# Weight blocks stored contiguously in memory and loaded from GpSimd's queue

## The chip, the cores and the metric

The kernel runs on one core of a Trainium2 chip. The metric is the device time of one execution in microseconds; lower is better. The profile shows the engines by short names: PE is TensorE's matmul, PEld its weight load, DVE is VectorE, ACT is ScalarE, POOL is GpSimd, and SP is the sync engine, which computes nothing and starts transfers. Every engine works through its own row of instructions in order and waits where an operand or a buffer isn't ready.

## The reference

The model is a trunk of two layers over 1024 tokens of 1024 channels in float32. Layer 0 mixes the tokens by an RG-LRU and a gated DeltaNet side by side (the even mixer), layer 1 by HGRN2 and RWKV-7 (the odd mixer). Each layer then has a gated feed-forward net and a gated embedding term:

```python
for layer in range(2):
    hn = rms_norm(h, norm_mix[layer])
    h = h + mixer(hn @ w_in[layer]) @ w_out[layer]        # even or odd
    f = rms_norm(h, norm_ffn[layer])
    h = h + (silu(f @ ffn_w_gate[layer]) * (f @ ffn_w_up[layer])) @ ffn_w_down[layer]
    g = sigmoid(rms_norm(h, norm_ple[layer]) @ ple_w_gate[layer])
    h = h + g * (p[layer] @ ple_w_up[layer])
return rms_norm(h, norm_final)
```

The weights e_w_in, e_w_out, o_w_in, o_w_out, the three of the feed-forward net and the two of the embedding term are the large ones. All products are to float32's accuracy.

## The kernel before

The tokens are worked on in two halves of 512. A large product is made from weight blocks of 128 x 1024 floats (8 tiles of 128 channels by 128 columns; in ffn_w_down 4 or 3 tiles of channels by 256 columns; 512 KB, twelve of them 384 KB). There are 450 blocks over the program. `weights` (line 1168) allots the tile wraw for a block (three buffers) and loads it by `load` (line 151), that is, from SP's queue. The weight lies in memory as the reference has it, so a block is 1024 pieces of 512 bytes, 8 for each of 128 partitions (for ffn_w_down pieces of 1 KB). Then the block is split: ACT copies it to whi, which holds the high part (line 304), and DVE subtracts that and leaves the low part in wlo (two buffers each). `products` (line 1182) multiplies each operand, itself split (xhi, xlo for the normed input; ghi, glo in the feed-forward net), in three passes: high by high, low by high, high by low. One pass of 128 x 128 weights over 512 tokens is one matmul of PE.

The order of each engine's row is set when the program is built. Every instruction gets a planned time (`at`, `clock`: loads 28,700 of the planner's units ahead of the product, splits 40,000), and a list scheduler with a model of the engines and queues picks the next instruction for each engine by it. So a change of a transfer's modelled time or queue can move instructions on all engines. The mixers of one half are spread over the dense products of another stage and fill the row of PE between them with small products, whose outputs are called mx.

Both mixers contain the inverse of many triangular 32 x 32 blocks (`invert_blocks`, line 480; eight times in the program, four for DeltaNet and four for RWKV-7). Their blocks are written to memory (scr, from aq or pm), and one load of 512 KB brings them back as lane, with one small system on each partition; L copies of a system lie on L partitions, so the source has a broadcast dimension. DVE then eliminates step by step (w<-lane,cols and cols<-cols,w), and the result goes through memory once more (invt) to the products that use it (`gdn_inverse`, line 511, and `r7_inverse`). Small transfers of all kinds (z, the mixers' inputs and outputs; up, the embedding term; hspill) use SP's queue too, in one row with the weights.

Of the kernel before, what the change touches and what calls it, by code (L numbers as in the profile page):

```python
# [19 lines left out]
P = 128  # L20
D = 1024
KD = D // P
# [6 lines left out]
# Planned times order the instructions: a pass of 512 tokens through the array takes PASS, the dense stages  # L29
# run from START on, and what they need is planned ahead of them by  # L30
PASS, START = 216, 100000
FETCH, WSPLIT = 28700, 40000    # weights: load, split
SPLIT, EARLY = 12000, 60000     # a mixer's output and other inputs
EVAC = 45000                    # what takes products out of the accumulators
# the second half's first operands; starts and ends of the mixers, against the dense stages around them
# [3 lines left out]
# a mixer's matrix products against its other instructions, and more behind a way through memory  # L39
LAG, ILAG = 7000, 4000  # L40
# shares and numbers of instructions of the parts of a mixer
# [18 lines left out]

class Trunk:
    def __init__(self, ctx, tc, ins, out):
        self.tc, self.nc = tc, tc.nc
        self.ins, self.out = ins, out
        self.const = ctx.enter_context(tc.tile_pool(name="const", bufs=1))
# [34 lines left out]
    def at(self, t, step=0, lag=0):  # L100
        """What follows is issued as if planned for time t, each instruction `step` after the last,
        and matrix products `lag` later, when their operands have long been there."""
        self.tc.cur_priority = max(int(t), 1)
        self.step, self.lag = step, lag
# [50 lines left out]
    def first_constants(self):  # L155
# [9 lines left out]
        # le[s, t] = 1 where s <= t  # L165
# [11 lines left out]
    def columns(self, stacks):  # L177
        """Per-channel vectors: rows of 128 channels, turned into columns."""
# [32 lines left out]
    def even_constants(self):  # L211
# [10 lines left out]
        # softplus(-lambda) = max(-lambda, 0) + ln(1 + exp(-|lambda|)), times 4  # L222
# [17 lines left out]
    def level_mask(self, m, dt):  # L240
        """mask[s, t] = 1 where s lies in the left half and t in the right half of the same block of 2m."""
# [6 lines left out]
        # 0 <= s - 2m*b < m  # L248
# [8 lines left out]
    def odd_constants(self):  # L257
# [13 lines left out]
        # takes the mean of a head's channels off  # L271
        self.cen = c.tile([P, P], F32, name="cen")
        self.stt(self.cen, self.blk, -1.0 / 64, self.ident, ALU.mult, ALU.add)
        # running sums start anew at every chunk
# [5 lines left out]
        # rows: k (64), beta (64); columns: alpha (s < t), r (s <= t)  # L280
# [9 lines left out]
    def rsqrt(self, x, y, t):  # L290
        """y = x ** -0.5, by exp and ln and one Newton step; t is scratch."""
        self.act(y, x, AF.Ln)
        self.act(y, y, AF.Exp, scale=-0.5)
        self.newton(x, y, t)

    def newton(self, x, y, t):
        """One step towards y = x ** -0.5."""
        self.mul(t, x, y)
        self.stt(t, t, -0.5, y, ALU.mult, ALU.mult)
        self.stt(y, t, 1.5, y, ALU.add, ALU.mult)  # L300

    def split(self, src, hi, lo):
        """src = hi + lo, both with the 12 bit significands that one pass of the array carries."""
        self.nc.scalar.copy(hi, src)  # L304
        self.sub(lo, src, hi)

    def rsqrt_cols(self, x):
        """x ** -0.5 of a few columns: half the exponent off the float's integer, then Newton steps."""
# [7 lines left out]
    def inv_mean(self, ps, n, scale, eps):  # L316
        """(scale * sum + eps) ** -0.5 of n columns of sums."""
# [5 lines left out]
    def load_unit(self, z, g, u, halo, tag):  # L323
        """Tokens of one unit with `halo` earlier ones of a group of four channel tiles."""
# [14 lines left out]
    def conv(self, x, w, bias, out):  # L339
        """Causal convolution, tile by tile; w: columns of tap k and tile j."""  # L340
# [12 lines left out]
    def rg_unit(self, z, u, mixed):  # L353
        """In steps, between which other work is issued."""
# [3 lines left out]
        c = self.w4()  # L358
# [15 lines left out]
        # with s = tanh(-log_a / 2): sqrt(1 - a^2) = sqrt(s) (1 + a); half of it, as gelu comes doubled  # L374
# [43 lines left out]
    def gdn_gates(self, ab):  # L418
        """Per half: columns over the tokens of a chunk, [token, chunk, head]."""
# [37 lines left out]
    def conv_silu(self, z, grp, u, out):  # L457
        """Twice silu of the convolved group, into out."""
# [10 lines left out]
    def head_norm(self, src, sq, dst, scale, eps):  # L469
        """dst = src * (scale * sum of sq + eps) ** -0.5, the sums over the 64 channels of a head."""  # L470
# [40 lines left out]
    def gdn_inverse(self, at, side):  # L511
        """Transposed inverses of I + A, at: [s, (chunk, head), t] with the transposes of the strictly lower A."""
# [24 lines left out]
        # pairs of 32: rows 32.. of the first and 96.. of the second  # L537
# [69 lines left out]
    def gdn_unit(self, z, u, cl, mixed, side):  # L607
        """Keys and queries stay as they leave silu (doubled); their norms are factors of the tokens."""
# [14 lines left out]
        # columns [token, chunk, head]  # L623
# [31 lines left out]
        # r * (r^2 mean(o^2) + eps)^-1/2 with r the query's factor, 1/sqrt(d) in it  # L655
# [26 lines left out]
    def gdn_scores(self, c, cc, kq, ks, cl, rk, kdc, aq):  # L682
        """aq: [s, head, (A | q k), t] with the decays exp(gc_t - gc_s), t >= s."""
# [32 lines left out]
    def gdn_chunk(self, c, ks, vb, nbe, o, tinv, qk, qe, kd, egl):  # L716
        """The recurrence over chunks; o: [token, head, channel]."""
# [45 lines left out]
    def hg_unit(self, z, u, mixed):  # L763
# [22 lines left out]
        # scores across the middles of blocks of 2m, by factors that reach to the middle  # L786
        for m in (64, 32, 16, 8, 4, 2, 1):
# [11 lines left out]
            # only the right halves of the blocks receive, in columns [block, token]  # L799
# [14 lines left out]
            else:  # L814
                # one product to a block: sums over the channels, on all partitions
# [78 lines left out]
    def r7_unit(self, z, u, mixed):  # L894
# [9 lines left out]
        # decay: log w = -KAPPA * (1 + tanh(.))  # L904
# [15 lines left out]
        # factors between chunks: exp(b_end - b_mid + next b_mid), and exp(b_mid) at the start  # L920
# [20 lines left out]
        # k * (1 + (a - 1) k_a)  # L941
# [5 lines left out]
        # bonus  # L947
# [56 lines left out]
    def r7_chunk(self, c, ar, bk, v, gs, o, pm, tinv, first):  # L1004
        """The recurrence over chunks; heads of pm and tinv in the order of (parity, pair)."""
# [50 lines left out]
    def fetch(self, hf, spare=False):  # L1056
        """The residual stream of a half, channels on partitions; spare: in the mixers' space."""
# [22 lines left out]
    def first_fetch(self, w):  # L1080
        """The first half of the input and its operands: h, and h * w in two parts."""
# [28 lines left out]
    def norm_scale(self, acc_tile=None):  # L1110
        """The inverse root mean squares of the tokens, on all partitions."""
# [18 lines left out]
    def norm(self, w):  # L1130
        """Operands h * w; the factors of the tokens (norm_scale) go to the products instead."""
# [9 lines left out]
    def even_operands(self, hf, w, alloc):  # L1141
        """Operands of the first projection: the input, normed with tokens on partitions."""
# [25 lines left out]
    def weights(self, w, k0, nk, c0, n):  # L1168
        """One block: raw, and its two parts, [channel, k, column]."""
# [6 lines left out]
        self.load(raw, w[P * k0:P * (k0 + nk), c0:c0 + n].rearrange("(k p) c -> p k c", p=P))  # L1176
# [5 lines left out]
    def products(self, w, k0, nk, c0, n, *sets):  # L1182
        """Yields w[k0.., c..]^T times the operands of each set for each 128 of n columns, to float32's
        accuracy in three passes."""
# [291 lines left out]
```

## Time and profile before

| | us |
|---|---|
| median of 3 runs | 3081.62 (3079.82 to 3084.49) |
| span of the profiled execution | 3078.0 |
| PE busy | 2972.8 (97%) |
| DVE busy | 1958.5 (64%) |
| ACT busy | 1264.2 (41%) |
| POOL busy | 27.5 (1%) |
| mean share of the 16 DMA engines that is busy | 38.8% |

The busy shares are means over the whole span. Times in the trace's views count from the span's start. Behind a row of a timeline stands in brackets how long the engine had been idle ahead of it and what it had waited for; a view of waits sums these idle times. A view of windows gives for a stretch the busy time of the engines, the granted clock of TensorE, the share of the DMA engines that is busy, and the rate.

### The profile page before, as it was taken

Reading aid. Unit: us, or ns where it says so; the run is one execution under the profiler, and the core shown is the slowest. Engines: PE = TensorE matmul, PEld = TensorE weight load, DVE = VectorE, ACT = ScalarE, POOL = GpSimd, SP = SyncE. Lnnn points to the kernel's source line nnn. Section 1 sums busy time; section 2 is a strip of 40 time slices with the busy share of each in tenths; the row PEclk is TensorE's granted clock in tenths of the full one; section 3 lists DMA queues with packets and bytes.
Section 4 is the critical chain, followed back from the end, with each engine's and each line's share of the span. In section 5 each row is a group of like instructions: output and inputs, shape, how many; then the busy total and the mean of one; then the engine's idle time right before and its main releaser. Section 6 shows DMA issues by size and latency. Waiting matters only on the chain.

```text
span 3078.0 us, 39136 instructions
## 1 busy us (share of the span) xinstructions
PE 2972.8 (97%) x15281; PEld 2407.9 (78%) x15281; DVE 1958.5 (64%) x3316; ACT 1264.2 (41%) x1799; POOL 27.5 (1%) x99
## 2 busy tenths in 40 slices
PE   8989899999999999999999999999998999999998
PEld 6878678778878887777877778777787787888886
DVE  5665556556676547745786574565687398555557
ACT  5344554233244436234443452442453355422224
POOL 0000000000000000000000000000000000000000
PEclk9999999999999999999999999999999999999999
DMA  6553663333234554222233444523233235333323
GB/s 207 146 140 110 167 202 100 111 86 103 84 110 137 164 167 149 86 78 91 86 107 93 131 143 136 162 86 79 83 110 89 53 96 181 100 120 99 97 89 103
DMA packets 547423, 360.18 MB, mean 117 GB/s; under 512 B 67287, under 2 KB 508806, under 8 KB 547238
## 3 DMA queue, kind: packets, MB, share of 16 engines
q1 hardware_dynamic: 547238, 357.68, 38.8%
q8 instruction: 120, 1.97, 0.3%
q14 instruction: 65, 0.53, 0.1%
HBM read 298.87 MB, written 58.75 MB: 116 GB/s over the span
## 4 chain that ended last, share of the span: by engine, by line
PE 55%; DVE 7%; DMA 3%; ACT 2%; issue 2%; SPq 0%; ACTq 0%; DVEq 0%
PE acc L144 46%; PE mx L144 8%; DMA lane<-scr 2%; DVE wlo L118 1%; DVE tmp L118 1%; PE mx L149 1%; DVE w L118 1%; DVE pm L118 1%; ACT w L139 1%; DVE w L131 0%; DMA tmp<-mixed 0%; DVE h L131 0%; DVE w L760 0%; ACT whi L304 0%; DVE tmp L131 0%
## 5 line engine op out<-in xcount | busy, mean ns | idle before, releaser
L144 PE MATMUL acc<-xhi,wlo 128*128 128x512 f32 x2864 | 1127.5, 394 | 18.9 <-DVE wlo L118 18.8
L144 PE MATMUL acc<-xhi,whi 128*128 128x512 f32 x2864 | 1137.4, 398 | 4.1 <-ACT xhi L304 2.9
L144 PE MATMUL acc<-xlo,whi 128*128 128x512 f32 x2864 | 1129.6, 395 | 1.0 <-DVE xlo L118 0.9
L304 ACT CAST whi<-wraw 128x1024 fp32r<-128x1024 f32 (+1 forms) x450 | 463.5, 1030 | 1157.1 <-PE acc L144 833.2
L144 PEld LDWEIGHTS acc<-xhi,wlo 128*128 128x128 f32 x2864 | 539.1, 188 | 139.3 <-DVE wlo L118 22.7
L144 PEld LDWEIGHTS acc<-xhi,whi 128*128 128x128 f32 x2864 | 539.4, 189 | 123.4 <-ACT xhi L304 5.4
L144 PEld LDWEIGHTS acc<-xlo,whi 128*128 128x128 f32 x2864 | 539.5, 188 | 119.5 <-issue 4.4
L118 DVE TENSOR_TENSOR wlo<-wraw,whi 128x1024 fp32r<-128x1024 f32 (+1 forms) x450 | 539.4, 1199 | 101.2 <-ACT whi L304 86.9
L118 DVE TENSOR_TENSOR tmp<-acc,rs 128x512 f32<-128x512 f32 (+1 forms) x205 | 140.8, 689 | 363.0 <-PE acc L144 362.6
L144 PE MATMUL acc<-ghi,wlo 128*128 128x512 f32 x704 | 278.7, 396 | 11.1 <-DVE wlo L118 11.1
L144 PE MATMUL acc<-ghi,whi 128*128 128x512 f32 x704 | 281.1, 400 | 2.6 <-ACT whi L304 2.5
L144 PE MATMUL acc<-glo,whi 128*128 128x512 f32 x704 | 277.8, 395 | 0.0
L144 PEld LDWEIGHTS acc<-ghi,wlo 128*128 128x128 f32 x704 | 134.0, 190 | 41.3 <-DVE wlo L118 12.9
L118 DVE TENSOR_TENSOR tmp<-tmp,acc 128x512 f32<-128x512 f32 x88 | 60.4, 686 | 166.4 <-PE acc L144 165.8
L144 PEld LDWEIGHTS acc<-ghi,whi 128*128 128x128 f32 x704 | 134.0, 191 | 32.7 <-ACT whi L304 2.9
L144 PEld LDWEIGHTS acc<-glo,whi 128*128 128x128 f32 x704 | 134.1, 190 | 28.0 <-DVE glo L118 0.6
L139 ACT ACTIVATE w<-w 128x1024 f32<-128x1024 f32 (+2 forms) x116 | 108.6, 940 | 105.3 <-DVE w L118 44.8
L131 DVE SCALAR_TENSOR_TENSOR h<-acc,h 128x512 f32<-128x512 f32 x144 | 98.6, 687 | 66.8 <-PE acc L144 66.3
L139 ACT ACT_TABLE_LOAD x83 | 106.5, 1283 | 5.5 <-DVE w L135 4.1
L118 DVE TENSOR_TENSOR w<-lane,cols 128x30 f32<-128x30 f32 (+43 forms) x248 | 57.5, 232 | 79.7 <-DMA lane<-scr 73.6
L139 ACT ACTIVATE tmp<-tmp 128x512 f32<-128x512 f32 x120 | 75.4, 629 | 54.8 <-DVE tmp L118 54.1
L304 ACT CAST ghi<-tmp 128x512 fp32r<-128x512 f32 x88 | 54.5, 619 | 100.8 <-DVE tmp L118 100.5
(320 smaller groups left out, 2729.0 us busy)
## 6 DMA issues: line engine op xcount, KB each, us to landing
wraw<-in_ffn_w_gate_dram SPq DMA_DIRECT2D x88, 512.0 KB
wraw<-in_ffn_w_up_dram SPq DMA_DIRECT2D x88, 512.0 KB
wraw<-in_ffn_w_down_dram SPq DMA_DIRECT2D x64, 512.0 KB
wraw<-in_o_w_in_dram SPq DMA_DIRECT2D x60, 512.0 KB
wraw<-in_e_w_in_dram SPq DMA_DIRECT2D x48, 512.0 KB
wraw<-in_ple_w_gate_dram SPq DMA_DIRECT2D x32, 512.0 KB
wraw<-in_ffn_w_down_dram SPq DMA_DIRECT2D x32, 384.0 KB
wraw<-in_e_w_out_dram SPq DMA_DIRECT2D x16, 512.0 KB
```

Source lines behind the costliest of these rows:

```text
L118: (eng or self.nc.vector).tensor_tensor(out, a, b, op=op)
L131: self.nc.vector.scalar_tensor_tensor(out, a, s, b, op0=op0, op1=op1)
L139: self.nc.scalar.activation(out, a, f, **kw)
L144: self.nc.tensor.matmul(out, lhsT, rhs, start=start, stop=stop)
L149: self.nc.tensor.transpose(out, a, self.ident)
L304: self.nc.scalar.copy(hi, src)
```

## The change

The host lays each of the nine large weights out anew: block after block in the order in which the kernel loads them, and within a block partition by partition, so that what goes to one partition is one piece of 4 KB (3 KB in the small blocks). `WEIGHTS` lists the blocks, the class `Weights` finds a block's offset, and the load in `weights` reads it as one flat stretch. This load is issued by `nc.gpsimd.dma_start`, from GpSimd's queue; `load`, and so every other transfer, stays with SP. Constants, buffers and planned times are as before; comments are taken out, which moves the line numbers (load is line 201, the weight load line 1226).

```diff
+def column_blocks(nk, n):
+    per = P * (KD // nk)
+    return [(b0, min(per, n - b0)) for b0 in range(0, n, per)]
+
+def in_blocks(order, groups, tails):
+    return [(0, KD, 512 * groups.index(g) + b0 if g in groups else 512 * len(groups) + b0, nb)
+            for g in order for b0, nb in column_blocks(KD, tails.get(g, 4 * P))]
+
+def plain_blocks(nk, n, k0=0, c0=0):
+    return [(k0, nk, c0 + b0, nb) for b0, nb in column_blocks(nk, n)]
...
+class Weights:
+    def __init__(self, ap, blocks):
+        self.ap, self.at, o = ap, {}, 0
+        for k0, nk, c0, n in blocks:
+            self.at[k0, nk, c0, n] = o
+            o += P * nk * n
+
+def laid_out(w, blocks):
+    import numpy as np
+    return np.stack([np.concatenate([
+        l[P * k0:P * (k0 + nk), c0:c0 + n].reshape(nk, P, n).transpose(1, 0, 2).ravel()
+        for k0, nk, c0, n in blocks]) for l in w])
...
         raw = block("wraw", F32, 3)
-        self.load(raw, w[P * k0:P * (k0 + nk), c0:c0 + n].rearrange("(k p) c -> p k c", p=P))
+        o = w.at[k0, nk, c0, n]
+        self.nc.gpsimd.dma_start(raw, w.ap[o:o + P * nk * n].rearrange("(p k c) -> p k c", p=P, c=n))
         self.at(self.clock - WSPLIT)
...
         a = np.ascontiguousarray(inputs[name])
+        if name in WEIGHTS:
+            a = laid_out(a, WEIGHTS[name])
```

The rows of the engines change in their order too. SP's row goes from 904 to 454 entries, POOL's from 85 to 535. On PE, ACT and DVE the same instructions stand in a slightly different order. Three places matter below.

The first is ACT's row at the start of the program, where the operands of the first half (xhi) are made from the transposed input (mx, acc), h is copied aside, and the first two weight blocks (whi_220, whi_251) are split. Before:

```order
L304 CAST whi_220<-wraw_218 128x1024
L139 ACTIVATE xhi_124<-mx_119,cols_95 128x512
...
L1099 COPY h_150<-mx_141 128x512
L139 ACTIVATE xhi_201<-mx_196,cols_95 128x512
L304 CAST whi_251<-wraw_249 128x1024
```

Now:

```order
L188 ACTIVATE xhi_124<-mx_119,cols_95 128x512
...
L188 ACTIVATE xhi_190<-acc_185,cols_95 128x512
L188 ACTIVATE xhi_201<-mx_196,cols_95 128x512
L353 CAST whi_220<-wraw_218 128x1024
L1148 COPY h_172<-acc_163 128x512
L353 CAST whi_251<-wraw_249 128x1024
```

The split of the first block has moved from the head of the row to behind the eighth operand. On PE the second block's first products (acc_255<-xhi_124,whi_251) have moved from the twentieth and twenty-first place of the dense products to the third and fourth.

The second place is PE's row in a stretch of the feed-forward net, where mx_3629 is the first small product on what DeltaNet's third elimination (w, brought back from memory) gives, between the dense products acc. Before:

```order
L144 MATMUL acc_6194<-glo_6078,whi_6190 128x512
L144 MATMUL acc_6194<-ghi_6077,wlo_6191 128x512
L144 MATMUL mx_3629<-w_624_3615,aq_3460 32x32 x8
L144 MATMUL acc_6208<-ghi_5722,whi_6190 128x512
L144 MATMUL acc_6208<-glo_5723,whi_6190 128x512
```

Now:

```order
L193 MATMUL acc_6174<-ghi_5931,wlo_6157 128x512
L193 MATMUL acc_6174<-ghi_6004,whi_6156 128x512
L193 MATMUL mx_3629<-w_624_3615,aq_3460 32x32 x8
L193 MATMUL acc_6174<-glo_6005,whi_6156 128x512
L193 MATMUL acc_6174<-ghi_6004,wlo_6157 128x512
```

It has moved up past the twelve products of acc_6194 and the last of acc_6174.

The third place is SP's row at the first lane load of RWKV-7. Before:

```order
L152 DMA scr_9393<-pm_9380 32x8x32 x2
L152 DMA lane_9402<-scr_9393 128x1x1024
L152 DMA wraw_11862<-in_ffn_w_down_dram 128x4x256
L152 DMA wraw_11896<-in_ffn_w_down_dram 128x4x256
L152 DMA wraw_11930<-in_ffn_w_gate_dram 128x8x128
```

Now:

```order
L201 DMA scr_9393<-pm_9380 32x8x32 x2
L201 DMA lane_9402<-scr_9393 128x1x1024
L201 DMA invt_9473<-colst_9471 1024x1x32 x2
```

The weight blocks behind the lane have left SP's row; they stand on POOL, in a row of nothing but weights.

## Rows read from the trace of the kernel before

**Rows 1.** The page, engines: busy time, share of the span, instructions.

```profile
PE 2972.8 (97%) x15281; PEld 2407.9 (78%) x15281; DVE 1958.5 (64%) x3316; ACT 1264.2 (41%) x1799; POOL 27.5 (1%) x99
```

**Rows 2.** Waits of PE: us in total, times, longest.

```profile
PE acc L144 <- DVE wlo L118: 29.9, 10, 6.9
PE mx L144 <- DVE w L131: 8.9, 1, 8.9
PE mx L144 <- issue: 8.5, 1, 8.5
...
PE acc L144 <- ACT whi L304: 3.6, 3, 2.5
...
PE acc L149 <- DMA tmp<-in_p_dram: 2.6, 2, 2.3
```

**Rows 3.** Waits of ACT before it splits a weight block.

```profile
ACT whi L304 <- PE acc L144: 833.2, 263, 11.3
...
ACT whi L304 <- DMA wraw<-in_e_w_in_dram: 9.3, 2, 7.3
```

**Rows 4.** Timeline of SP's queue: start and duration in us of each issue.

```profile
22.10 0.43 SPq L152 DMA_DIRECT2D wraw<-in_e_w_in_dram  x1
...
845.49 1.81 SPq L152 DMA_DIRECT2D scr<-aq  x4
849.59 0.39 SPq L152 DMA_DIRECT2D wraw<-in_ffn_w_down_dram  x1
...
1263.21 0.57 SPq L152 DMA_DIRECT2D lane<-scr  x1
1267.67 0.40 SPq L152 DMA_DIRECT2D wraw<-in_ffn_w_down_dram  x1
...
3001.04 0.37 SPq L152 DMA_DIRECT2D wraw<-in_ple_w_gate_dram  x1
```

**Rows 5.** Timeline of ACT: the start, and one later split.

```profile
9.40 1.04 ACT L304 CAST whi<-wraw 128x1024 fp32r<-128x1024 f32 x1 [7.31 <-DMA wraw<-in_e_w_in_dram]
...
15.44 0.72 ACT L139 ACTIVATE xhi<-mx,cols 128x512 fp32r<-128x512 f32 x1
...
26.58 1.04 ACT L304 CAST whi<-wraw 128x1024 fp32r<-128x1024 f32 x1 [2.01 <-DMA wraw<-in_e_w_in_dram]
...
3010.70 1.05 ACT L304 CAST whi<-wraw 128x1024 fp32r<-128x1024 f32 x1
```

**Rows 6.** Timeline of DVE behind the first lane load of RWKV-7.

```profile
1276.63 0.19 DVE L118 TENSOR_TENSOR w<-lane,cols 128x31 f32<-128x31 f32 x1 [8.39 <-DMA lane<-scr]
...
1280.05 1.22 DVE L118 TENSOR_TENSOR wlo<-wraw,whi 128x1024 fp32r<-128x1024 f32 x1
```

**Rows 7.** Timeline of PE at the start, in the feed-forward net, behind that lane.

```profile
14.28 0.47 PE L144 MATMUL acc<-xhi,whi 128*128 128x512 f32 x1
...
27.68 0.50 PE L144 MATMUL acc<-xhi,whi 128*128 128x512 f32 x1 [0.62 <-ACT whi L304]
...
644.43 0.69 PE L144 MATMUL mx<-w,aq 32*32 32x32 f32 x16 [0.73 <-DVE w L522]
...
1276.00 0.39 PE L144 MATMUL acc<-glo,whi 128*128 128x512 f32 x1
1281.32 0.80 PE L144 MATMUL acc<-ghi,wlo 128*128 128x512 f32 x1 [4.93 <-DVE wlo L118]
```

**Rows 8.** Windows, PE alone, behind that stall: busy (instructions), clock, DMA share, GB/s.

```profile
1281.40:1286.40 5.00, 5.00 (x12) 0.50 0.31 105
```

**Rows 9.** The page, DMA queues: packets, MB, share of 16 engines.

```profile
q1 hardware_dynamic: 547238, 357.68, 38.8%
```

**Rows 10.** Windows, two lane loads (DeltaNet, RWKV-7): busy of each engine, clock, share, GB/s.

```profile
313.65:325.75 12.10, 8.47 (x38) 6.68 (x36) 1.12 (x2) 1.87 (x3) 0.00 (x0) 0.96 0.83 151
1276.00:1277.50 1.50, 0.39 (x2) 0.00 (x0) 0.77 (x4) 0.00 (x0) 0.00 (x0) 1.00 0.13 44
```

More of the change, by code (lines that the diff above doesn't have):

```diff
@@ L58 @@
 )
+def column_blocks(nk, n):
[6 more added lines that the diff above has]
+    return [(k0, nk, c0 + b0, nb) for b0, nb in column_blocks(nk, n)]
+FSTARTS = [sum(FCHUNKS[:c]) for c in range(len(FCHUNKS))]
+WEIGHTS = {
+    "e_w_in": in_blocks(EVEN_ORDER, EVEN_GROUPS, {"ab": 8}),
+    "o_w_in": in_blocks(ODD_ORDER, ODD_GROUPS, {"wag": 2 * P}),
+    "e_w_out": plain_blocks(KD, D),
+    "o_w_out": plain_blocks(KD, D),
+    "ffn_w_gate": [b for k0, nk in zip(FSTARTS, FCHUNKS) for b in plain_blocks(KD, P * nk, 0, P * k0)],
+    "ffn_w_up": [b for k0, nk in zip(FSTARTS, FCHUNKS) for b in plain_blocks(KD, P * nk, 0, P * k0)],
+    "ffn_w_down": [b for k0, nk in zip(FSTARTS, FCHUNKS) for b in plain_blocks(nk, D, k0)],
+    "ple_w_up": plain_blocks(2, D),
+    "ple_w_gate": plain_blocks(KD, D),
+}
+class Weights:
[9 more added lines that the diff above has]
+        for k0, nk, c0, n in blocks]) for l in w])
 class Trunk:
@@ L64, in __init__ @@
         self.ins, self.out = ins, out
+        self.w = {n: [Weights(ins[n][l], b) for l in range(ins[n].shape[0])] for n, b in WEIGHTS.items()}
         self.const = ctx.enter_context(tc.tile_pool(name="const", bufs=1))
@@ L1182, in products @@
     def products(self, w, k0, nk, c0, n, *sets):
-        per = P * (KD // nk)
-        for b0 in range(0, n, per):
-            nb = min(per, n - b0)
+        for b0, nb in column_blocks(nk, n):
             hi, lo = self.weights(w, k0, nk, c0 + b0, nb)
@@ L1239, in ffn @@
     def ffn(self, ops, wg, wu, wd, side=None):
-        starts = [sum(FCHUNKS[:c]) for c in range(len(FCHUNKS))]
+        starts = FSTARTS
         cols = [[self.products(w, 0, KD, P * k0, P * nk, ops) for w in (wg, wu)] for k0, nk in zip(starts, FCHUNKS)]
@@ L1285, in ple_up @@
                 pops[-1].append(op)
-        ups = self.products(self.ins["ple_w_up"][layer], 0, 2, 0, D, *pops)
+        ups = self.products(self.w["ple_w_up"][layer], 0, 2, 0, D, *pops)
         for hf in halves:
@@ L1296, in ple @@
         rs = None
-        for m, g in enumerate(self.products(self.ins["ple_w_gate"][layer], 0, KD, 0, D, ops)):
+        for m, g in enumerate(self.products(self.w["ple_w_gate"][layer], 0, KD, 0, D, ops)):
             if rs is None:
@@ L1397, in block @@
             c = slice(KD * layer, KD * layer + KD)
-            self.ffn(self.norm(self.cols["norm_ffn"][:, c]), *(ins[n][layer] for n in ("ffn_w_gate", "ffn_w_up", "ffn_w_down")), side=side)
+            self.ffn(self.norm(self.cols["norm_ffn"][:, c]), *(self.w[n][layer] for n in ("ffn_w_gate", "ffn_w_up", "ffn_w_down")), side=side)
             self.ple(self.norm(self.cols["norm_ple"][:, c]), layer, up[layer, hf])
@@ L1403, in odd_in @@
             ops = self.norm(nm[:, KD:2 * KD])
-            self.project_in(hf, ins["o_w_in"][0], ops, ODD_ORDER, ODD_GROUPS, z[1], self.norm_scale)
+            self.project_in(hf, self.w["o_w_in"][0], ops, ODD_ORDER, ODD_GROUPS, z[1], self.norm_scale)
         e, o = 25 * 24 * PASS, 30 * 24 * PASS
@@ L1418, in run @@
         self.put(0)
-        self.project_in(0, ins["e_w_in"][0], ops, EVEN_ORDER, EVEN_GROUPS, z[0], lambda: self.norm_scale(self.bank))
+        self.project_in(0, self.w["e_w_in"][0], ops, EVEN_ORDER, EVEN_GROUPS, z[0], lambda: self.norm_scale(self.bank))
         self.at(START + X0)
         ops = self.even_operands(1, nm, spare)
-        self.project_in(1, ins["e_w_in"][0], ops, EVEN_ORDER, EVEN_GROUPS, z[0])
+        self.project_in(1, self.w["e_w_in"][0], ops, EVEN_ORDER, EVEN_GROUPS, z[0])
         self.at(START - 20000)
@@ L1431, in run @@
         self.odd_constants()
-        block(0, 0, ins["e_w_out"][0])
+        block(0, 0, self.w["e_w_out"][0])
         odd_in(0)
         self.odd_mixer(0, z[1], mixed[1], t[4] + ODD_SPAN[0][0], t[6] + ODD_SPAN[0][1])
-        block(0, 1, ins["e_w_out"][0])
+        block(0, 1, self.w["e_w_out"][0])
         odd_in(1)
@@ L1441, in run @@
             self.load(self.wfinal[i], ins["norm_final"][512 * i:512 * i + 512].unsqueeze(0).broadcast_to([P, 512]))
-        block(1, 0, ins["o_w_out"][0])
-        block(1, 1, ins["o_w_out"][0], spare=True, side=self.final(0, self.h))
+        block(1, 0, self.w["o_w_out"][0])
+        block(1, 1, self.w["o_w_out"][0], spare=True, side=self.final(0, self.h))
         for _ in self.final(1, self.h):
```

## The prediction

> **What bounds the kernel now.** The engine table comes first: TensorE is busy 2972.8 of the 3078.0 us of the span [rows 1]. It takes its instructions in their written order, so only what shortens or lengthens its idle time, about 105 us by subtraction, can move the end. The waits of PE say what that idle time is [rows 2]: 29.9 us in 10 waits for wlo, the low part of a weight block; single waits of 8.9 and 8.5 us for the mixers' products; 2.6 us for an embedding load. None names a weight transfer. The waits of the other engines confirm it: ACT, which splits each block first, waited 833.2 us for PE to give a whi buffer free, and 9.3 us in two waits for a block to land [rows 3]. A block on the way takes about 4.5 us where something waits for it (issued at 22.10, split at 26.58) [rows 4, 5], and behind the first eight blocks the shortest time from issue to split is 9.7 us (3001.04 to 3010.70) [rows 4, 5]; so about 5 us can be lost before the split is late. Cheaper weight transfers in themselves are worth next to nothing.
>
> Where PE does wait for wlo, the long ones stand behind the lane loads of RWKV-7, of which there are four. At 1263.21 SP issues lane, at 1276.63 DVE gets it, 8.39 us after it ran out of work [rows 4, 6]. DVE's row has four lane steps and more ahead of the wlo of a block that PE wants, so that starts at 1280.05 [rows 6], and PE, whose last matmul ends at 1276.39, stands until 1281.32 [rows 7]. The other three stalls of this kind are as long or longer, up to 6.9 us [rows 2]. Behind such a stall the granted clock is 0.50 for the next 5 us, in which 12 matmuls go through [rows 8].
>
> **Part 1: packets.** Rows of 512 bytes become rows of 4 KB, 128 for a block in place of 1024. All of the kernel's 547,238 packets hold 38.8% of 16 engines for 3078 us, 35 ns each [rows 9]. At that mean, 1024 packets cost 36 us of engine time, 2.2 us on 16 engines; a lane load of RWKV-7, alone and in 4 KB pieces, shows a share of 0.13, two engines of sixteen, and 44 GB/s [rows 10], 22 GB/s each, so 4 KB take 0.19 us and a new block 128 x 0.19 / 16 = 1.5 us. It saves 0.7 us per block on engines that are busy 39% of the time: nothing, except where a transfer that ends a stall lies behind weights. That is so at the four lane loads of DeltaNet, with an engine share of 0.83 and 151 GB/s (313.65 to 325.75) [rows 10]; one or two blocks share each of them. The price is 0 to -2 us for each, 0 to -8 in all; I take -2, as the two long stalls behind them (8.9 and 8.5) [rows 2] wait for whole chains of steps, of which the load is one.
>
> **Part 2: the queue.** SP loses 450 issues, POOL gains them. SP's order held other transfers behind waiting weights for some 280 us, but nearly all of these are not waited for by PE. Two are: the embedding load that ends a wait of 2.3 us at 416, part of [rows 2], and the lane of 850.15, whose scr writes were issued by 847.3 while SP stood until 849.59 for a wraw buffer [rows 4]. Gains up to 2.3 each; behind the lane PE stands for 2.5 us, for an ACT step, so I take -1 for the lane and -2 for the other. On POOL a weight's wait holds up only memsets and masks, with 85 instructions in the whole program, and none of them comes late to a reader by the times of before.
>
> POOL's own cost of starting a load isn't in this trace. The lower bound is SP's 0.37 to 0.43 us of issue [rows 4], which is no later; the upper bound, as it must not stop everything, is the 5 us of slack, in which it would still cost nothing outside the start. I take nothing.
>
> **Part 3: lanes of RWKV-7 beside weights.** One or two weight blocks are issued around each of these four lanes (at 1267.67, 4.5 us behind the lane) [rows 4]. In SP's queue they stood behind it; now they come through a queue of their own while only 2 of 16 engines carry the lane. If the two engines share turns, 8 packets of the block lie among the lane's 64: 8 x 0.19 = 1.5 us, all of it on the path lane, DVE, wlo, PE. So 0 to 6 us for four; below nothing is possible only for the block that stood ahead (1612.59), by the same 1.5. The row nearest to it, the lane's own 22 GB/s, says an engine has one packet's worth of speed to share; I take +4.
> The Trainium skill ("DMA: Bandwidth & Descriptors", section "Queues, rings and completion order") says that a DMA engine goes round the queues it has work for and drains a packet from one before it takes the next. By it the block's share is done beside the lane, the term is +6, and the sum 2 us higher; no run here has two loading queues yet.
>
> **Part 4: the start.** Before, ACT split the first block at 9.40, ahead of all operands, and dense work began at 14.28 [rows 5, 7]. After, ACT's row has that split behind the eighth operand xhi_201, which ended at 16.16 [rows 5], then a copy, then the second block's split; and PE's third and fourth dense product want that second block. With 0.7 for the copy, as for xhi_201: 16.16 + 1.04 + 0.7 + 1.04 = 18.9, less two products already done (0.5): the dense stage starts 4.1 us later. The third block, awaited before (ACT idle to 26.58, PE for 0.62 at 27.68 and as much again) [rows 5, 7], is then long there: -1.2. Net +2.9; up to 5 if three blocks beside 2 MB of x bring x 1 us later and the 1.2 isn't gained, down to 0 if the mixers' later stalls swallow the delay. I take +2.5.
>
> **Part 5: products moved in PE's row.** The scheduler's new transfer times move some mixer products up. Their operands were just in time: mx_3629 at 644.43 waited 0.73 us [rows 7] and now stands 15 matmuls (3.4 us) earlier. Four more, whose operands also came within a microsecond of them, stand 5 to 13 matmuls (1.1 to 3 us) earlier. If no operand comes sooner: 3.4 + 4 x 1.7 = 10.2. If they do, since SP holds no transfer back: 0. As the stages behind mx_3629 were waited for anyway, a wait taken early is partly given back; I take +2.
>
> **Sum.** -2 (packets) -1 -2 (queue) +4 (lanes) +2.5 (start) +2 (moved products) = +3.5 on 3078.0: 3081.5. The median of the runs lies 3.6 above that span: **3085**. A measurement here can tell about 0.2% (6.2 us) from no change, so this is "within": 3075.5 to 3087.8. Own range of this case: 3079 to 3091.
>
> **Rivals.**
> *Slower: lanes and moved products in full.* Place: the four RWKV-7 stalls (+6), the moved products at their bound (+10), the start (+4), gains as above at half (-2.5): +17.5, about 3099. For: PE's rows are fixed, and a product that waits stops everything behind it; against: most moved products were planned so because their transfers come earlier. It decides from 4 us of the moved products' 10 on, with the lanes whole.
> *Faster: DeltaNet's chain.* With SP free and the engines lighter, scr, lane, invt and zin of DeltaNet each start and land sooner. Four lanes at -2 = -8, both queue gains -4.6 (2.3 each), start 0, lanes of RWKV-7 0, and a moved product nowhere late: -12.6, about 3069. For: engine share 0.83 under these lanes; against: lanes of 12 us are long because of their own size.
> *Hidden anyway.* No term is real, and the start's delay is swallowed: 3078 to 3082, inside "within". The Trainium skill (same page, "Issuing engines are not separate DMA queues") has this rule: transfers started from any engine run on the same 16 engines and only the issue time is saved. Here 450 x 0.37 us of issue lie on SP, which nobody waits for.
> *Weights late.* If POOL takes over 5 us more for a block than SP did, each later microsecond falls on up to 450 splits: 1 us beyond costs hundreds. Nothing in the rows points at it.
>
> **Chances.** Forecast and "hidden anyway" inside the bound: 0.42. Slower: 0.33 (the first rival and the upper part of the forecast's own range 0.29, weights late 0.04). Faster: 0.25 (second rival and lesser forms of it). The range takes both ends in: 3069 below, 3101 above (3099 with the start at its 5 and a little for one new half-clock stretch).
>
> **What would show it.** Right: dense work from about 18.4 us on; no wait of ACT for wraw behind the start; RWKV-7 lanes about 1 us longer from issue to DVE, and PE's waits for wlo around 32 us; a PE wait at mx_3629 of 2 us or more. Wrong: waits of ACT for wraw all along (weights late); DeltaNet lanes of 9 to 10 us and stalls at 183 and 322 under 7 (faster); dense work at 14 us as before.

## The result and the profile after

The changed kernel takes 3114.3 us in the median of its runs (3105.7 to 3117.9), the kernel before 3081.4 (3079.8 to 3084.5). The ratio of the two kernels is 1.0098, with a 95% interval of 1.0086 to 1.0110; the medians lie 32.9 us apart. It is one per cent slower, outside the predicted range of 3069 to 3101. The profiled execution spans 3115.9 us, 37.9 more than before. It is the longest of its kernel's four. Executions of one kernel lie up to 17 us apart here, and the longer ones have the lower granted clock (3105.7 us at 0.981, 3117.9 at 0.976); so what a single profile says of one place holds only to some us.

The page of the changed kernel, engines and DMA queues, answers to [rows 1] and [rows 9]:

```profile
PE 2984.6 (96%) x15281; PEld 2418.4 (78%) x15281; DVE 1958.7 (63%) x3316; ACT 1263.3 (41%) x1799; POOL 266.5 (9%) x549
...
q0 software_dynamic: 62528, 230.78, 24.2%
q1 hardware_dynamic: 135558, 126.90, 12.9%
```

q0 is GpSimd's queue with the weights, q1 SP's with all the rest; together they hold the engines for 37.1%, where it was 38.8%. The same matmuls keep PE busy for 11.8 us longer (the mean granted clock went from 0.982 to 0.976), and PE's idle time grew by 26.1 us (3115.9 - 2984.6, less 105.2). The two make up the 37.9.

The waits of PE in the changed kernel (total, times, longest) say what the idle time is for, beside [rows 2]:

```profile
PE acc L193 <- DVE wlo L167: 37.3, 9, 8.1
PE mx L193 <- issue: 9.5, 1, 9.5
PE acc L193 <- ACT whi L353: 8.4, 4, 5.2
PE mx L193 <- DVE w L180: 7.7, 1, 7.7
PE mx L198 <- DMA w<-in_x_dram: 7.2, 4, 4.0
PE acc L198 <- DMA tmp<-in_p_dram: 6.6, 3, 3.8
PE mx L193 <- DVE w L571: 6.0, 4, 3.9
```

No row names a weight block on its way. The waits behind lanes (wlo, whi) grew by 12 us, those for x and for the embedding by 8 (x: 3.3 to 7.2, in_p: 2.6 to 6.6), and those for the inverse brought back from memory (w) went from 0.7 to 6.0.

As PE does the same dense products in nearly the same order, the start of a dense product after, less that of the same product before, shows where the time is lost:

| place (time in the kernel before, us) | distance grows by |
|---|---|
| start, to 45 | 7.1 |
| 45 to 588 | 0 (some up, some down) |
| 588 to 620: third DeltaNet lane | 4.2 |
| 620 to 650: mx_3629 and the products behind it | 7.2 |
| 843 to 877: fourth DeltaNet lane | 3.3 |
| around the four RWKV-7 lanes | 0.9, 1.7, 2.3, 0.9 |
| 2397 to 2470: behind the fourth of them | 6.9 |
| all others | 2.5 |
| end | 37.0 |

Two kernels further down have the same rows at these places, but for the start, and load all weights or all but three blocks from GpSimd's queue ("the queue alone" and "the start"). In their profiles the lanes cost as much as here: 4.3 and 4.3 us at the third DeltaNet lane, 3.5 and 2.9 at the fourth, about 6 around the four of RWKV-7. Two rows don't repeat: the one of mx_3629 costs 4.0 and 1.7 in place of 7.2, and the stretch behind the fourth RWKV-7 lane 0 and 3.0 in place of 6.9.

The first RWKV-7 lane, to be read beside [rows 4, 6, 7]; timelines of SP, POOL, DVE and PE, and the row of the DMA view for the block that came beside it (KB, us from issue to landing):

```profile
1286.13 0.58 SPq L201 DMA_DIRECT2D lane<-scr  x1
...
1290.97 0.53 POOL L1226 DMA_DIRECT2D wraw<-in_ffn_w_down_dram  x1 [11.48 <-DVE wlo L167]
...
wraw<-in_ffn_w_down_dram POOLq DMA_DIRECT2D x1, 512.0 KB, 8.0
...
1300.92 0.19 DVE L167 TENSOR_TENSOR w<-lane,cols 128x31 f32<-128x31 f32 x1 [9.65 <-DMA lane<-scr]
...
1305.61 0.80 PE L193 MATMUL acc<-ghi,wlo 128*128 128x512 f32 x1 [6.19 <-DVE wlo L167]
```

From issue to DVE the lane takes 14.8 us, before 13.4; PE stands for 6.2 us, before 4.9. The block beside it lands after 8.0 us, where 3.8 is the median. Nobody waits for the block. The DMA view counts the packets of the two queues. From 1295.5 to 1298.3 us, while the lane and the end of the block are on the way:

```profile
q1 hardware_dynamic: 20, 0.08, 7.2%
q0 software_dynamic: 17, 0.07, 5.8%
```

and in the kernel before, from 1271 to 1276 us, with the lane by itself:

```profile
q1 hardware_dynamic: 66, 0.26, 13.0%
```

Both times the share is 13% of 16 engines, that is, two of them. Before, they carried nothing but the lane; now nearly half of their packets are the block's.

### The profile page after: what moved, and what is told of

Read it like the earlier page. It is cut to its first block, busy times and chain, and to the rows that moved or that the text cites. A ratio compares the mean times of both kernels' runs of the same rounds, so it can differ in the third digit from the quotient of the medians.

```text
span 3115.9 us, 39309 instructions
## 1 busy us (share of the span) xinstructions
PE 2984.6 (96%) x15281; PEld 2418.4 (78%) x15281; DVE 1958.7 (63%) x3316; ACT 1263.3 (41%) x1799; POOL 266.5 (9%) x549
## 4 chain that ended last, share of the span: by engine, by line
PE 75%; DVE 11%; DMA 7%; ACT 3%; issue 3%; SPq 1%; POOL 0%; ACTq 0%; DVEq 0%
PE acc L193 62%; PE mx L193 11%; DMA lane<-scr 2%; DVE wlo L167 2%; DVE w L167 2%; DVE tmp L167 1%; PE mx L198 1%; DVE w L180 1%; DVE cols L167 1%; SPq L201 1%; ACT w L188 1%; DMA tmp<-mixed 1%; DMA invt<-colst 1%; ACT whi L353 1%; DVE pm L167 1%
## 5 line engine op out<-in xcount | busy, mean ns | idle before, releaser
L1226 POOL DMA_DIRECT2D wraw<-in_ffn_w_down_dram x96 | 51.0, 531 | 634.7 <-DVE wlo L167 607.7
```

Source lines behind the costliest of these rows:

```text
L1226: self.nc.gpsimd.dma_start(raw, w.ap[o:o + P * nk * n].rearrange("(p k c) -> p k c", p=P, c=n))
```

## The experiments

The layout and the queue can be set apart with no change of order: with the new layout on SP's queue, the rows of PE, ACT, DVE and SP are those of the kernel before; with the old layout on GpSimd's queue they are those of the changed kernel. Theory A is the one of the prediction's third part, taken further: weights in a queue of their own share the DMA engines with the mixers' transfers, and these are what PE waits for. Rivals are the layout (B), the order of the rows (C) and, for the start, that later stalls swallow it (D).

**The layout alone.**

```diff
-        self.nc.gpsimd.dma_start(raw, w.ap[o:o + P * nk * n].rearrange("(p k c) -> p k c", p=P, c=n))
+        self.load(raw, w.ap[o:o + P * nk * n].rearrange("(p k c) -> p k c", p=P, c=n))
```

> The new layout alone: weight blocks stored contiguously, loaded from SP's queue as in the kernel before. The rows of PE, ACT, DVE and SP are those of the kernel before, so only the packets differ (4 KB in place of 512 B). Theory A (the separate queue: weights and the mixers' transfers share the DMA engines, the way through memory gets longer, and PE, whose row is fixed, waits): RWKV-7 lanes from issue to DVE 13.1 to 13.8 us as before, and a time within 0.3% of before (3073 to 3091). Rival B (the layout: a packet of 4 KB holds an engine longer than eight of 512 B do and delays others): lanes of 14.3 us and more, and 3100 to 3120.

Measured: 3074.0 us (3071.3 to 3077.5, ten runs), a ratio of 0.9985 to the kernel before (0.9976 to 0.9995). The layout by itself is a small gain. The page's queue row, and the lane's first step on DVE (lane issued at 1261.05, so 13.3 us):

```profile
q1 hardware_dynamic: 200358, 357.68, 36.5%
...
1274.32 0.19 DVE L167 TENSOR_TENSOR w<-lane,cols 128x31 f32<-128x31 f32 x1 [8.28 <-DMA lane<-scr]
```

Rival B falls. The packets fall to 200,358, but the share of the engines from 38.8% to 36.5% only: 73 us of all 16 engines, 0.16 us for each of 450 blocks.

**The queue alone.** The kernel before, with `self.load` in `weights` made `self.nc.gpsimd.dma_start`.

> The queue alone: the weights as in the reference's layout (512-byte rows), loaded from GpSimd's queue. The rows of PE, ACT, DVE and SP are those of the changed kernel. Theory A (queue): slow as the changed kernel, 3100 to 3125, RWKV-7 lanes 14.3 us or more. Rival B (layout): near before, 3075 to 3095, lanes near 13.4. If GpSimd's cost of a load goes by the number of rows (1024 in place of 128), its issue would take several us and the time would lie far above both, 3130 or more.

Measured: 3115.8 us (3112.6 to 3118.4), ratio 1.0118 (1.0099 to 1.0138), the four RWKV-7 lanes 14.4 to 16.3 us. All of the loss comes with the queue and the order that goes with it, none with the layout.

**One stretch, with the order held.** Only blocks 180 to 259 from GpSimd's queue; PE, ACT and DVE keep the rows of the kernel before.

```diff
+        self.nw += 1
+        q = self.nc.gpsimd if 180 <= self.nw < 260 else self.nc.sync
-        self.nc.gpsimd.dma_start(raw, ...)
+        q.dma_start(raw, ...)
```

> The new layout, with blocks 180 to 259 (about 1235 to 1760 us) from GpSimd's queue and all others from SP's. The rows of PE, ACT and DVE are those of the kernel before, word for word, so only the queue differs, in the stretch of the first two RWKV-7 lanes. Theory A1 (transfers of two queues share the engines): these two lanes take 14.2 to 15.5 us from issue to DVE (layout alone: 13.3 and 13.8), the stalls behind them about 6.0 and 7.0 us (4.8 and 5.3), the last two lanes stay at 13.1 to 13.3; time 2 to 6 us over the layout alone, 3075 to 3081. Rival C (order): nothing changes, 3072 to 3076.

Measured: SP's issues and DVE's first steps of the first two RWKV-7 lanes, and PE's stall behind the first:

```profile
1256.16 0.57 SPq L201 DMA_DIRECT2D lane<-scr  x1
1270.64 0.19 DVE L167 TENSOR_TENSOR w<-lane,cols 128x31 f32<-128x31 f32 x1 [9.55 <-DMA lane<-scr]
1275.33 0.79 PE L193 MATMUL acc<-ghi,wlo 128*128 128x512 f32 x1 [6.10 <-DVE wlo L167]
...
1606.82 0.56 SPq L201 DMA_DIRECT2D lane<-scr  x1
1622.54 0.19 DVE L167 TENSOR_TENSOR w<-lane,cols 128x31 f32<-128x31 f32 x1 [9.85 <-DMA lane<-scr]
```

The two lanes take 14.5 and 15.7 us (layout alone: 13.3 and 13.8), the two behind them, with weights on SP's queue, 13.2 and 13.1. Over these two places the distance to the layout alone grows by 1.4 and 2.4 us. The time is 3079.3 us (3073.4 to 3085.8), ratio 1.0004 (0.9991 to 1.0017), where the layout alone has 0.9985. With the order the same, theory A1 holds at these places.

**Which queue.** The same blocks from ACT's queue; and the other way round, all weights from SP's queue and only the first two RWKV-7 lanes from GpSimd's.

```diff
-        q = self.nc.gpsimd if 180 <= self.nw < 260 else self.nc.sync
+        q = self.nc.scalar if 180 <= self.nw < 260 else self.nc.sync
```

> The new layout, blocks 180 to 259 loaded from ACT's queue, all others from SP's: a second queue that isn't GpSimd's. ACT's row and PE's change somewhat in that stretch. If any second queue lets weights in beside the lane: the first two RWKV-7 lanes take 14.2 us or more from issue to DVE, the last two 13.0 to 13.5. If it is GpSimd's queue alone: all four 13.0 to 13.9.

```diff
-        self.load(self.flat(at), src.unsqueeze(0).broadcast_to([L, nb, B * B]))
+        (self.nc.gpsimd if self.nl in (5, 6) else self.nc.sync).dma_start(
+            self.flat(at), src.unsqueeze(0).broadcast_to([L, nb, B * B]))
```

> The new layout with all weights from SP's queue, and the first two RWKV-7 lane loads alone from GpSimd's; the rows of PE, ACT and DVE are those of the kernel before. If the two queues take turns on the lane's engines whichever of them carries the lane: these two lanes take 14.2 to 15.8 us, as with the weights from GpSimd's queue. If GpSimd's queue is served ahead of SP's: 13.4 or less.

The first lane's issue and first step, weights on ACT's queue, and then the lane on GpSimd's:

```profile
1256.74 0.57 SPq L201 DMA_DIRECT2D lane<-scr  x1
1271.57 0.19 DVE L167 TENSOR_TENSOR w<-lane,cols 128x31 f32<-128x31 f32 x1 [9.38 <-DMA lane<-scr]
```

```profile
1267.44 0.92 POOL L538 DMA_DIRECT2D lane<-scr  x1 [79.47 <-DMA scr<-pm]
1282.33 0.19 DVE L167 TENSOR_TENSOR w<-lane,cols 128x31 f32<-128x31 f32 x1 [10.46 <-DMA lane<-scr]
```

14.8 and 14.9 us; the second lanes 14.6 and 15.1; the lanes left on SP's queue with the weights 12.8 to 13.5. It isn't GpSimd: the two queues take turns on the lane's engines, whichever carries the lane. The Trainium skill ("DMA: Bandwidth & Descriptors", section "Queues, rings and completion order") says so of the engines, and these runs agree: the four lanes are 0.8 to 1.6 us longer than with the layout alone, where eight packets were put at 1.5. Of the lane on GpSimd's queue some 0.4 us can be its issue, 0.92 us long where SP's takes 0.57. (One run each, 3069.4 and 3082.9 us; their times decide nothing.)

**The third DeltaNet lane and the moved product.** Blocks 78 to 91 from GpSimd's queue; with it the scheduler moves mx_3629 up as in the changed kernel.

> The new layout, with blocks 78 to 91 (about 580 to 650 us) from GpSimd's queue, the others from SP's. PE's row differs from the kernel before in one place: mx_3629 and the first of mx_3639 stand where the changed kernel has them, 15 dense products earlier. Theory A1: the third DeltaNet lane takes 12.5 to 13.5 us (layout alone 10.8) and the stall at 599 grows from 1.7 to 5 us or more. With the moved product, the stall at 644 is 2.5 to 4 us and a half-clock stretch follows; time 3080 to 3088. Rival C (order alone): lane and stall at 599 as with the layout alone, the stall at 644 about 4 us, 3077 to 3082.

Measured: 3078.7 us (3075.8 to 3083.3), ratio 1.0004 (0.9992 to 1.0016). The lane, issued at 587.96, and the stall behind it:

```profile
601.24 0.19 DVE L167 TENSOR_TENSOR w<-lane,cols 128x31 f32<-128x31 f32 x1 [11.47 <-DMA lane<-scr]
...
604.57 0.80 PE L193 MATMUL acc<-xhi,wlo 128*128 128x512 f32 x1 [5.59 <-DVE wlo L167]
```

13.3 us in place of 10.8 and a stall of 5.6 in place of 1.7: as expected, and 5.4 us are lost here in this profile. But not all of it is the queue's. DVE's row differs at this place too, as it does in the changed kernel, which the expectation left out: wlo stands behind four lane steps, where it was two. From the first step to wlo in the kernel before (and as long with the layout alone), and here:

```profile
599.17 0.19 DVE L118 TENSOR_TENSOR w<-lane,cols 128x31 f32<-128x31 f32 x1 [9.16 <-DMA lane<-scr]
600.28 1.22 DVE L118 TENSOR_TENSOR wlo<-wraw,whi 128x1024 fp32r<-128x1024 f32 x1
```

```profile
603.29 1.22 DVE L167 TENSOR_TENSOR wlo<-wraw,whi 128x1024 fp32r<-128x1024 f32 x1
```

1.1 us before, 2.05 now: of the 3.9 us by which the stall grew, some 0.9 are the order's. And the stall at mx_3629 did not come: it waits 0.50 us, a product behind it 0.76. With this kernel's timing the product stands early and its operand is there. The time lies below the expected 3080 to 3088 and inside rival C's 3077 to 3082; it doesn't tell the two apart, the lane does.

**The same, with the product put back.** The planned lag of that inverse's products is 8 us longer.

```diff
-        self.lag = lag + ILAG
+        self.ng += 1
+        self.lag = lag + ILAG + (8000 if self.ng == 3 else 0)
```

> As the kernel with blocks 78 to 91 from GpSimd's queue, but the products on the third DeltaNet inverse (mx_3629 and those behind it) get 8 us more lag in the planned times, so they stand no earlier in PE's row than in the kernel before. It tells the queue from the order at that place. If the moved product is what stalls PE at 644: that stall is below 1 us and no half-clock stretch follows, and the time is 4 to 8 us below that of the kernel without the lag. If the late transfers alone do it: the chain is late all the same, a stall of 2 us or more shows up at the new place, and the time is within 2 us of it.

Measured: 3071.6 us, with runs from 3067.8 to 3082.2, ratio 0.9978 (0.9963 to 0.9994); in the profile this place is passed 4.4 us quicker than with the moved product, although the stall at 599 is as long (6.0). The medians are 7 us apart, in the expected sense, but the runs overlap, so the order's share here is 4 to 7 us by these two kernels and not better known.

**The start.** The first three blocks from SP's queue again, the others from GpSimd's.

> The changed kernel with the first three weight blocks loaded from SP's queue again, between the x tiles as in the kernel before; the first 180 entries of PE's row are then those of the kernel before, the rest is as in the changed kernel. Theory A: the changed kernel's start is late because x waits beside three blocks and the rows of ACT and PE put the first split behind all operands; with this edit dense work starts at 14 to 15 us (changed kernel: 19), and the time falls by 5 to 8 us, to 3103 to 3110. Rival D: the mixers' stalls at 183 and 322 us swallow the late start, and the time stays at 3110 to 3118.

Measured: 3103.8 us (3098.4 to 3115.9), ratio 1.0091 (1.0058 to 1.0125). The first dense product, in this kernel and then in the changed one, where it is preceded by waits for x:

```profile
15.51 0.49 PE L193 MATMUL acc<-xhi,whi 128*128 128x512 f32 x1
```

```profile
9.47 0.47 PE L198 MATMUL mx<-ident,w 128*128 128x128 f32 x1 [4.00 <-DMA w<-in_x_dram]
11.42 3.04 PE L198 MATMUL mx<-ident,w 128*128 128x128 f32 x13 [1.48 <-DMA w<-in_x_dram]
...
19.52 0.70 PE L193 MATMUL acc<-xhi,whi 128*128 128x512 f32 x1 [2.38 <-ACT whi L353]
```

At 45 us the distance to the kernel before is 1.3 us in place of 7.1, and it isn't swallowed later: at 588 us the kernel is 0.5 us ahead of the kernel before, the changed one 7.2 behind. So rival D falls by the profile. The times are less sharp: the medians differ by 10.5 us, but the runs overlap (the ratios are 1.0091 and 1.0098). Runs with the same granted clock differ as the profile has it: at 0.977, 3106.9 us here, 3113.0 and 3115.7 in the changed kernel.

**Lane loads on all engines.** One load with a broadcast dimension outermost becomes L loads of one copy.

```diff
-        self.load(self.flat(at), src.unsqueeze(0).broadcast_to([L, nb, B * B]))
+        for q in range(L):
+            self.load(self.flat(at)[nb * q:nb * q + nb], src)
```

On the changed kernel:

> The changed kernel, with each lane load made as L loads (4 for DeltaNet, 2 for RWKV-7) of one copy each, so that no broadcast dimension stands outermost and all DMA engines can carry it. Theory A: the extra time comes mainly by way of the lane loads, so lanes fall to 5 to 8 us from issue to DVE, the stalls behind them (5.8, 5.2, 6.2, 7.1, 8.1, 6.8 us in the changed kernel) fall below 2 us with their half-clock stretches, and the time to 3055 to 3085. Rival C (the order: instructions of PE, ACT and DVE were moved up, whatever the transfers take): the lanes get shorter but products moved up still wait, and the time stays above 3095.

On the kernel before:

> The kernel before, with the lane loads made the same way. Theory A: the stalls behind the lanes (2.3, 2.5, 4.9, 5.3, 6.9, 5.9 us) and the half-clock stretches behind them go, 3035 to 3060; the distance to the changed kernel with the same edit is what the start and the other transfers cost, 10 to 25 us. Rival C: the same distance of 33 us remains between the two.

Measured: 3045.8 us (3044.8 to 3048.7) and 3025.7 (3023.5 to 3027.3), ratios 0.9893 and 0.9825, both below what theory A expected (3055 to 3085 and 3035 to 3060). In the second, the first RWKV-7 lane (two issues), the DMA share and rate in the stretch behind them, and DVE's first step:

```profile
1235.70 1.65 SPq L152 DMA_DIRECT2D lane<-scr  x2
...
1235.70:1239.00 3.30, 3.30 (x17) 2.72 (x16) 1.85 (x3) 1.49 (x2) 0.00 (x0) 1.00 0.54 142
...
1240.26 0.19 DVE L118 TENSOR_TENSOR w<-lane,cols 128x31 f32<-128x31 f32 x1
```

A share of 0.54 where it was 0.13 (1271 to 1276 us in the kernel before), 4.6 us where it was 13.4, and DVE no longer idles for it; PE's long waits for wlo are gone in both kernels. The Trainium skill ("DMA: Bandwidth & Descriptors", section "Why a DMA increments its semaphore by 16 and not by 1") has the rule that the outermost dimension sets how many engines share a transfer; the 2 of 16 before and the fall here agree. With the long lanes gone the two kernels are 20.1 us apart, as theory A had it (10 to 25), where it was 30 (by the ratio) to 33 (by the medians); so 10 to 13 us of the loss went by way of the lanes. The edit does more than shorten the lanes, though: the scheduler places instructions anew for it, and in about one of eight places of PE's row, and one of four of DVE's, another instruction stands. How much of the 53.1 us that the kernel before gains is this order, no run tells.

**What is left of the queue's cost, and the best of all.** Wide lanes and the first three blocks on SP's queue, the others on GpSimd's; and wide lanes with the new layout, all on SP's queue.

> The changed kernel with wide lane loads and its first three weight blocks from SP's queue: what GpSimd's queue still costs when the long lanes and the late start are gone. Against the same with all weights from SP's queue (the kernel beside it): if the cost went by lanes and start alone, both agree within 5 us; if other transfers on the mixers' way through memory, and products placed by the scheduler for faster transfers, carry a part of it, it is 10 to 20 us slower, 3030 to 3042.

> The new layout loaded from SP's queue, with each lane load made as L loads of one copy: the two edits that each lowered the time, together. If they add, as their causes are apart (fewer packets; a transfer on all engines in place of 2 or 4): 3025.7 less 4.7, 3015 to 3026. If the gain of the layout lay only in shorter lanes, which are short here already, nothing is left of it: 3023 to 3030.

Measured: 3031.5 us (3027.8 to 3041.1) and 3022.4 (3021.8 to 3029.5; ratio to the kernel before 0.9831, 0.9812 to 0.9850). Without long lanes and late start the queue, and the order that goes with it, still cost some 9 us, between the two expectations (the ratios' intervals, 0.9835 to 0.9880 and 0.9812 to 0.9850, just touch). The second kernel is faster than both kernels of this case; whether the layout adds something to wide lanes (3022 against 3026) these runs don't decide.

## Why the prediction was wrong

The step that failed is to count the sharing of the engines at the four RWKV-7 lanes alone. At DeltaNet's lanes and the other small transfers Parts 1 and 2 put down gains, 5 us in all; the third and fourth DeltaNet lanes took 13.3 and 13.9 us in place of 11.2 and 10.8, and 7.5 us were lost there. Beside it the start was mis-sized (7.1 us for 2.5), and the lower clock behind a new stall was no term of the sum.

**What bounds the kernel** held: PE's row, stalls for wlo behind lanes, weights well ahead. In no profile does PE wait for a weight block, and "weights late" was rightly the least of the rivals. That only PE's idle time could move the end did not hold: 11.8 of the 37.9 us are longer busy time.

**Part 1, packets (-2 at DeltaNet's lanes).** Mis-sized at "at that mean": the price of a 512-byte packet was taken from the mean of all packets. The layout alone showed 0.16 us saved per block, not 0.7. The price of 4 KB came from a misread row: in the second stretch of [rows 10] no lane is on the way. The DMA view of 1276 to 1277.5 us has

```profile
DMA packets 67, 0.07 MB, mean 44 GB/s; under 512 B 3, under 2 KB 67, under 8 KB 67
```

so no packet of 4 KB. These are pieces of 1 KB, of the block issued 4.5 us behind the lane, which were left over on the lane's two engines until the lane was through. The lane itself goes at 0.26 MB in 5 us, 52 GB/s (1271 to 1276 us), so 4 KB take 0.16 us and not 0.19, and the eight packets of Part 3 1.3 us and not 1.5. DeltaNet's lanes gained 0.3 us on average from the layout alone (12.3, 11.5, 10.8 and 10.5 us against 12.0, 12.1, 11.2 and 10.8).

**Part 2, the queue (-1 and -2).** Here the sign was wrong. The lane of 850 did start without the wait for a weight, but then took 13.9 us and not 10.8, and PE's stall behind it grew from 2.5 to 5.2; the longest wait for the embedding load grew to 3.8. What SP's row had held back was small beside what the weights take on the engines.

**Part 3, RWKV-7 lanes (+4).** Mechanism and size were right: the lanes take 14.8, 15.3, 14.4 and 14.4 us against 13.4, 13.7, 13.1 and 13.6, 1.3 us more in the mean, and the distance grows by 5.8 us there; by the eight packets it would be about 5. The error was to confine it. The same sharing can hit the other transfers on the mixers' way through memory. At DeltaNet's third and fourth lanes 7.5 us were lost (some 0.9 of them by DVE's order), where a gain was put down. And in some places the way back takes longer. Timelines of SP and POOL in the changed kernel, from the stores of the third DeltaNet inverse to the load that waits for them, and the product that waits for that:

```profile
643.94 2.81 SPq L201 DMA_DIRECT2D invt<-colst  x4
650.45 0.37 SPq L201 DMA_DIRECT2D w<-invt  x1
...
646.43 0.53 POOL L1226 DMA_DIRECT2D wraw<-in_ffn_w_down_dram  x1 [4.78 <-DVE wlo L167]
649.76 0.53 POOL L1226 DMA_DIRECT2D wraw<-in_ffn_w_gate_dram  x1 [2.80 <-DVE wlo L167]
...
655.12 1.05 PE L193 MATMUL mx<-w,aq 32*32 32x32 f32 x16 [3.94 <-DVE w L571]
```

The same of SP's row in the kernel before:

```profile
636.52 2.55 SPq L152 DMA_DIRECT2D invt<-colst  x4
639.17 0.55 SPq L152 DMA_DIRECT2D wraw<-in_ffn_w_gate_dram  x1
640.51 0.37 SPq L152 DMA_DIRECT2D w<-invt  x1
```

The load can go 6.5 us after the first store, where it was 4.0. It isn't so each time: in the kernel of "the start", with a block issued just as soon behind the first store, it goes after 4.0 us, in that of "the queue alone" after 4.4. At the first DeltaNet inverse it goes after 5.4 to 5.7 us in all three, where it was 4.2. So weights in a queue of their own can slow the way back; what made it 6.5 us here isn't shown. At the lanes SP's single row was a priority: what the chain needs first, weights after.

**Part 5, moved products (+2, bound 10).** The place named, mx_3629, did stall 3.9 us in this execution. With the same rows it stalls 1.5 us in the kernel of "the queue alone" and not at all in that of "the start"; with the product moved and blocks 78 to 91 alone from GpSimd's queue, 0.5. The place cost 7.2 us here, 4.0 and 1.7 in the first two. That the product stands earlier costs some us (4 to 7 by the pair above); the size here is in part this execution's luck.

**Part 4, the start (+2.5, at most 5).** Mis-sized: 7.1. The rows of ACT and PE were read rightly, but x itself came late: two waits of 4.0 and 1.5 us for x, with three blocks issued beside it by 3.80 us. The bound allowed x one microsecond. The idea that the mixers' later stalls would take the delay up was wrong too.

**The missing term: half clock.** A new stall isn't paid by its length alone. Behind the fourth RWKV-7 lane the way back takes longer too (5.9 us from store to load, before 3.7), and PE waits 1.2 us ahead of a product whose operand came in time before. Windows of PE (length, busy and instructions, clock, DMA share, GB/s) behind that stall and behind the one of mx_3629 in the changed kernel:

```profile
654.60:664.60 10.00, 9.48 (x43) 0.50 0.24 75
2436.30:2449.90 13.60, 13.60 (x123) 0.50 0.15 44
```

and the same stretches in the kernel before:

```profile
646.70:656.70 10.00, 9.70 (x74) 1.00 0.18 54
2406.00:2420.00 14.00, 14.00 (x171) 1.00 0.31 81
```

Behind the stall of 1.2 us PE ran 13.6 us at the lower of the two clocks, 1.2 GHz, and 6.9 us were lost there. But this is one execution. In the kernel of "the start" the same product waits longer, and only 3.4 us at the lower clock follow; 3.0 us are lost:

```profile
2420.73 1.17 PE L193 MATMUL mx<-m,pm 32*32 32x32 f32 x32 [1.65 <-DVE m L634]
...
2422.00:2425.40 3.40, 3.40 (x22) 0.51 0.48 125
```

In that of "the queue alone" it doesn't wait, and nothing is lost. So the length of the stretch doesn't follow from that of the stall, and what decides it stays open. Over the whole span PE's busy time grew by 11.8 us for the same matmuls. The prediction's sum had no term for it; only the range's upper end had "a little for one new half-clock stretch".

So the "slower" rival had the right side and, at the lanes, the right mechanism, but its price was half: DeltaNet's lanes (+7.5 in place of -5 with both queue gains), the start (+4.6 over), the two places behind ways back with their half clock (+14 where +2 stood; 4 to 5 in the two other profiles, so the last size is luck). What stays open is how the loss divides between sharing and order: no kernel had all weights in GpSimd's queue and the rows of the kernel before. The runs at single places show both, and the order's part could be bounded only to some us; the same goes for the 9 us that are left with wide lanes and the old start.

## What to carry to other kernels

Before transfers are spread over queues, ask which ones end a wait. If the bulk traffic has slack and small transfers on a chain have none, one queue in which the chain's stand ahead is worth more than the issue time it costs: bulk loads in a second queue take turns with them on the engines that both use. And look at how many engines carry a transfer that something waits for; here splitting one broadcast load by its outermost dimension, with the new order that came of it, gave 53 us on the kernel before, more than the change cost.

## What the runs showed of the hardware

With ACT's or GpSimd's queue as the second one, beside SP's, an RWKV-7 lane came 0.8 to 1.9 us later than with the layout alone, in two lanes of three kernels each. GpSimd's queue packs short rows: the page of the kernel with the old layout, whose rows are 512 bytes, shows packets of 3.6 KB on average for its weights:

```profile
q0 software_dynamic: 63552, 230.78, 24.9%
```

The layout shows in its own work: a load is started in 0.53 us and lands after 3.8 in the median with the new layout, 0.88 and 4.5 with the old one. In time it made no difference that the runs can tell (3115.8 against 3114.3 us), as no block is waited for.

Not expected either was how far a short stall can reach: 1.2 us of idle PE ahead of small products and 13.6 us at a granted clock of 0.50 behind it in one execution, 1.65 us and 3.4 at the same place in another.
